# Decays between the tokens of a chunk from running sums in a hybrid encoder block

## Chip, cores and metric

The kernel runs on one core of a Trainium2 chip. The metric is the device time of one execution in microseconds; the median of three runs is given. TensorE (PE in the profile) multiplies matrices into PSUM, VectorE (DVE), ScalarE (ACT) and GpSimd (POOL) work elementwise, and the queue of SyncE (SP) issues nearly all DMAs.

## What is computed

The reference is an encoder block for 2048 tokens of 1024 channels with two branches: a gated delta rule in both directions, and a long convolution. The change is in the delta rule. Per head and direction, g is the running sum of the tokens' log decays within a chunk, and every pair of tokens i >= j of the chunk has the decay exp(g_i - g_j):

```python
g = jnp.cumsum(g..., axis=-1)
diff = g[..., :, None] - g[..., None, :]
decay = jnp.where(tril, jnp.exp(jnp.where(tril, diff, 0.0)), 0.0)
a = jnp.where(strict, jnp.einsum("nhcid,nhcjd->nhcij", k_beta, k) * decay, 0.0) + eye
sol = triangular_solve(a, [v * beta, k_beta * exp(g)])
attn = jnp.einsum("nhcid,nhcjd->nhcij", q, k) * decay
# then a scan over the chunks with the state S: v_new = u - w S, o = q S + attn v_new, S = S g_last + k^T v_new
```

## The kernel before

All large products are f32 split into two parts (h and l, `fp32r`), three products each. The program goes through the normalised input, the second branch's projections with its filter, the gates (`gates_in`), the projections of the delta rule (`delta_in`), the merge gates (`gate_out`), the recurrence over the chunks (`chain`) and the output projections.

Projections: `products` (L595) makes one block of 128 columns for 512 tokens with 24 products of 128x512. A head of `delta_in` has three blocks of four quarters, 288 products. After each product `tick` advances a generator, the filler, once per `gran` products (8 in `delta_in` up to its last blocks, 4 behind them), and `wait(n)` lets at least n products pass. From `gates_in` on, TensorE executes this hand-written order; the other engines' orders are a scheduler's.

The filler there is `delta_prep`. For each of 8 heads it runs `corr`, `invert32` and `invert`, up to three heads at a time in turn; a head starts when its projections are done and `corr` of the head before is through. `corr` takes four groups of four chunks of 128 tokens. Per group: products of keys with keys (`pka`) and queries with keys (`pkb`, L899); diagonal and step sizes on VectorE (L905 to L911); then for both directions the decay `e`, which is multiplied with beta on GpSimd (`co`, L923) and with `pka` on VectorE (L924), cut into blocks and stored, masked on GpSimd (L933), multiplied with `pkb` on VectorE (L935) and stored. `e` itself is made of two masked copies of the decays, `gmh` on GpSimd and `gml` on VectorE (L915), a pause of 12 products, two products with a triangle of ones (`pd`, L919) that add the decays from j to i, and an exponential on ScalarE (L921). `invert32` inverts 32x32 blocks on VectorE (L954, L956), one row after the other. `invert` puts them together to chunks with five groups of products per four chunks (L992 to L1021), whose results go through `ptw` (ScalarE), `G`, `T` (VectorE) and copies on either (`evac`).

When the filler is through or a block of `gate_out` ends behind it, `chain` becomes the filler, at the same kind of pace over the remaining blocks of `gate_out`.

Of the kernel before, what the change touches and what calls it, by code (L numbers as in the profile page):

```python
# [11 lines left out]
F32 = mybir.dt.float32  # L12
# [10 lines left out]
H = 8  # L23
# [3 lines left out]
# per direction: (source, target) blocks of 32 rows, and halves of 64  # L27
# [54 lines left out]
def _consts():  # L82
# [70 lines left out]
class Ring:  # L153
    """Tiles that are kept for the whole phase and used in turn."""
# [11 lines left out]
class K:  # L166
# [13 lines left out]
    def tick(self):  # L180
        """Called per matrix product; work of the filler goes between the products."""
# [42 lines left out]
    def sin(self, pool, y):  # L224
        """y -> y reduced to [-pi, pi], in place."""
# [121 lines left out]
    def filt_freq(self, pp, rk_dram, kf_dram):  # L347
        """Spectrum of the filter, real parts over imaginary parts, one slot after the other."""
# [29 lines left out]
    def conv_freq(self, pp, ru_dram, kf_dram, r2_dram):  # L378
        """Product of the spectra and the way back to rows, N channels at a time."""
# [6 lines left out]
        with tc.tile_pool(name="cf", bufs=1) as cp:  # L386
# [3 lines left out]
            def fetch(i):  # L390
# [14 lines left out]
                else:  # L405
                    # row 0 of the first slot holds two real values
# [127 lines left out]
    def start(self, sz_dram, consts):  # L534
        """The normalised input, each part of the tokens used as soon as it is there."""
# [30 lines left out]
    def z_out(self, pool, h, q, ps, sz_dram):  # L566
        """silu(z) * norm weight."""
# [16 lines left out]
    def proj(self, pp, w, q):  # L584
        """One block of 128 columns for 512 tokens: [columns, tokens] in PSUM."""
# [12 lines left out]
    def conv_in(self, pool, tag, prev, ps, q, cw, out):  # L598
        """Takes a quarter out of PSUM; returns its tile and finishes the quarter before it."""
# [18 lines left out]
    def quarters(self, wp, pp, pool, src, cw, tag, done, w=None):  # L618
        """Projection and short convolution of one block; done(q, tile) gets each quarter."""
# [831 lines left out]
```

## Time and profile before

| | before |
|---|---|
| time, median of 3 runs | 3622.15 us (3622.11 to 3626.81) |
| profiled execution, span | 3631.3 us |
| busy: TensorE, VectorE, ScalarE, GpSimd | 94%, 61%, 39%, 42% |
| TensorE's granted clock, mean | 0.973 of 2.4 GHz |

The profiled execution is one run of the program; its span runs from its first to its last instruction. A busy time is the time in which at least one instruction of the engine is running. TensorE's products overlap, so a product's recorded duration is longer than its distance to the next one. A wait is named by the instruction that waited and the one that released it.

### The profile page before, as it was taken

What the parts mean: (1) busy time and instruction counts of PE and PEld (TensorE: products, weight loads), DVE (VectorE), ACT (ScalarE), POOL (GpSimd) and SP (SyncE); (2) the same over time, 40 slices, a digit from 0 to 9 for tenths busy, and PEclk for the clock granted to TensorE, in tenths of its full rate; (3) what the DMA queues carried; (4) which work ended last, traced back from release to release, by engine and by line L of the source; (5) the groups of instructions that cost most, each with busy time, mean ns of one, the idle gap of its engine ahead of it and who ended that gap; (6) DMA issues with size and microseconds to landing.
All of it is one profiled execution on the core that took longest, in us unless ns stands there. A gap on an engine that the chain in (4) does not pass through costs nothing. (4 is left out here: it accounts for less than half of the span.)

```text
span 3631.3 us, 57914 instructions
## 1 busy us (share of the span) xinstructions
PE 3398.0 (94%) x18300; PEld 2870.9 (79%) x18300; DVE 2229.7 (61%) x4847; ACT 1415.6 (39%) x3425; POOL 1535.4 (42%) x1899
## 2 busy tenths in 40 slices
PE   7999999999999988889999989899998888998999
PEld 6768888888887767777777778788887766888998
DVE  7596566555325687798887652455555599535433
ACT  3344444443223434444443332344444577413221
POOL 3235666676432443433443222433334587324210
PEclk9999999999999999999999999999999999999999
DMA  3343333475211345555555654676677688886442
GB/s 125 131 100 99 111 120 97 133 237 173 86 55 60 105 109 137 134 131 128 139 130 150 152 135 112 192 210 209 200 215 213 203 276 260 282 303 189 148 140 94
DMA packets 721609, 565.03 MB, mean 156 GB/s; under 512 B 251302, under 2 KB 616954, under 8 KB 720280
## 3 DMA queue, kind: packets, MB, share of 16 engines
q1 hardware_dynamic: 721160, 561.21, 53.7%
q8 instruction: 146, 2.39, 0.3%
q14 instruction: 159, 1.30, 0.1%
q0 software_dynamic: 144, 0.13, 0.0%
HBM read 342.96 MB, written 218.17 MB: 155 GB/s over the span
## 5 line engine op out<-in xcount | busy, mean ns | idle before, releaser
L595 PE MATMUL pj<-hh,wh 128*128 128x512 f32 (+1 forms) x2592 | 1042.8, 403 | 22.7 <-DVE wh L204 11.2
L595 PE MATMUL pj<-hl,wh 128*128 128x512 f32 (+1 forms) x2592 | 1039.7, 402 | 3.5 <-POOL hl L205 2.9
L595 PE MATMUL pj<-hh,wl 128*128 128x512 f32 (+1 forms) x2592 | 1038.9, 402 | 1.3 <-POOL wl L205 1.2
L595 PEld LDWEIGHTS pj<-hh,wh 128*128 128x128 f32 x2592 | 498.6, 193 | 116.4 <-DVE wh L204 13.3
L595 PEld LDWEIGHTS pj<-hl,wh 128*128 128x128 f32 x2592 | 499.0, 193 | 91.9 <-POOL hl L205 3.6
L595 PEld LDWEIGHTS pj<-hh,wl 128*128 128x128 f32 x2592 | 498.5, 192 | 91.6 <-issue 4.4
L205 POOL TENSOR_TENSOR wl<-wraw,wh 128x512 fp32r<-128x512 f32 x160 | 221.3, 1383 | 395.9 <-DVE wh L204 261.0
L1084 POOL TENSOR_SCALAR kvq<-kvq,kn 128x128 f32<-128x128 f32 x256 | 153.9, 610 | 300.0 <-DMA kvq<-kvq 81.5
L204 DVE CAST wh<-wraw 128x512 fp32r<-128x512 f32 x160 | 89.4, 559 | 158.2 <-DMA wraw<-in_wb 106.8
L1304 POOL TENSOR_TENSOR gt<-gt,ex 128x256 f32<-128x256 f32 x64 | 48.0, 750 | 190.1 <-issue 98.8
L915 POOL TENSOR_TENSOR gmh<-masks,gh 128x512 fp32r<-128x512 f32 x64 | 75.0, 1172 | 124.6 <-PE pd L919 108.1
L209 PE MATMUL pj<-rh,hh 128*128 128x256 f32 x448 | 126.7, 284 | 1.0 <-DVE gt L1303 0.9
L210 PE MATMUL pj<-rl,hh 128*128 128x256 f32 x448 | 126.8, 283 | 0.6 <-POOL rl L205 0.6
L211 PE MATMUL pj<-rh,hl 128*128 128x256 f32 x448 | 126.7, 283 | 0.0
L616 DVE SCALAR_TENSOR_TENSOR o<-h_p,chy,o 128x512 f32<-128x512 f32 x96 | 83.1, 876 | 70.7 <-POOL h_p L608 69.5
L1164 DVE SCALAR_TENSOR_TENSOR S<-S,gt,ch 128x128 f32<-128x128 f32 x224 | 69.1, 344 | 93.4 <-PE ch L1161 93.2
L205 POOL TENSOR_TENSOR fl<-f,fh 128x256 fp32r<-128x256 f32 x128 | 99.5, 781 | 61.1 <-DVE fh L204 61.0
L205 POOL TENSOR_TENSOR l<-raw,h 128x256 fp32r<-128x256 f32 x128 | 99.9, 793 | 42.2 <-DVE h L204 41.9
L205 POOL TENSOR_TENSOR hl<-oraw,hh 128x512 fp32r<-128x512 f32 x48 | 62.5, 1304 | 130.5 <-ACT hh L202 116.5
L204 DVE CAST h<-raw 128x256 fp32r<-128x256 f32 x128 | 68.1, 547 | 75.0 <-PE pk L211 50.8
L927 ACT ACTIVATE od<-co 32x128 f32<-32x128 f32 x256 | 78.5, 307 | 88.1 <-DVE co L924 74.6
L923 POOL TENSOR_TENSOR co<-e,beta 128x512 f32<-128x512 f32 x64 | 79.5, 1242 | 73.4 <-ACT e L921 54.4
(328 smaller groups left out, 8145.7 us busy)
## 6 DMA issues: line engine op xcount, KB each, us to landing
kvq<-kvq SPq DMA_DIRECT2D x256, 192.0 KB
wraw<-in_wb SPq DMA_DIRECT2D x160, 256.0 KB
ep<-ep SPq DMA_DIRECT2D x256, 128.0 KB
ru<-ev SPq DMA_DIRECT2D x64, 256.0 KB
rk<-ev SPq DMA_DIRECT2D x128, 128.0 KB
raw<-rk SPq DMA_DIRECT2D x128, 128.0 KB
kf<-ev SPq DMA_DIRECT2D x128, 128.0 KB
kvq<-th SPq DMA_DIRECT2D x64, 256.0 KB
```

The costliest lines, as they stand in the source:

```text
L204: (eng_h or nc.vector).tensor_copy(h, src)
L205: (eng_l or nc.gpsimd).tensor_tensor(l, src, h.bitcast(F32), op=ALU.subtract)
L209: nc.tensor.matmul(ps, lhsT=ah, rhs=bh, start=first, stop=False)
L210: nc.tensor.matmul(ps, lhsT=ah, rhs=bl, start=False, stop=False)
L211: nc.tensor.matmul(ps, lhsT=al, rhs=bh, start=False, stop=last)
L595: self.nc.tensor.matmul(ps, lhsT=a[:, k], rhs=b[k][:, ts_], start=k == 0 and j == 0, stop=k == 7 and j == 2)
L616: nc.vector.scalar_tensor_tensor(out, p[:, 2:514], cw[:, 2:3], out, op0=ALU.mult, op1=ALU.add)
L915: e.tensor_tensor(t, self.mi[d].rearrange("p (a b) -> p a b", a=1).broadcast_to(S4), col(v.bitcast(F32), d), op=ALU.mult)
L923: nc.gpsimd.tensor_tensor(o, e, col(self.an, d), op=ALU.mult)
L927: nc.scalar.activation(od[blk(b)], o[blk(b), :, blk(b)], AF.Copy)
L1084: nc.gpsimd.tensor_scalar(a[:, 1], a[:, 1], self.kn[:, h, c:c + 1], None, op0=ALU.mult)
L1164: nc.vector.scalar_tensor_tensor(Sn, St[d], self.gt[:, c, ci], ps[:, 2], op0=ALU.mult, op1=ALU.add)
```

## The change

`gates_in` now makes the running sums of the decays of all heads, chunks and both directions with one product each against the constant `mid` (sums counted from the middle token of the chunk), keeps them with tokens on partitions (`cum`), turns them, and stores them in DRAM (`cr`), one row of 128 tokens per chunk. In `corr`, `decay(g, d)` loads four chunks' rows to all 128 partitions, clips -(row - cum) at zero on ScalarE, one chunk per instruction since `cum` differs by chunk, and takes exp(-x). The decays of the first group are asked for before the head's first products, those of group g + 1 right behind the last use of those of group g. `e` has three buffers instead of one; the PSUM buffer of `pd` becomes a second one for the inversions. The masked copies, the products `pd` and the pause ahead of them are gone; the pause between the directions is 12 products instead of 1. The masks and g stay in plain f32.

```diff
+    c["mid"] = np.stack([le - le[:, 63:64], le.T - le.T[:, 64:65]], 1)
...
+            mid = dp.tile([128, 2, 128], F32, name="mid", bufs=1)
+            self.load(mid, A["mid"])
+            ps = tp.tile([128, 2, H, NCH], F32, name="pcum", tag="pt")
+            for d in range(2):
+                nc.tensor.matmul(ps[:, d], lhsT=mid[:, d], rhs=self.g[:, :, 8 * d:8 * d + 8].rearrange("p c h -> p h c"), start=True, stop=True)
+            nc.scalar.activation(self.cum, ps, AF.Copy)
+            pt = tp.tile([128, 2, 128], F32, name="pcr", tag="pt")
+            for d in range(2):
+                nc.tensor.transpose(pt[:, d], self.cum[:, d].rearrange("p h c -> p (h c)"), self.ident)
+            cr = dp.tile([128, 2, 128], F32, name="cr", bufs=1)
+            nc.scalar.activation(cr, pt, AF.Copy)
+            self.store(cr_dram.rearrange("d r t -> r d t"), cr)
...
-        self.split(self.gh, self.gl, y, eng_l=V)
+        V.tensor_copy(self.g, y)
...
+        def decay(g, d):
+
+            e = P.tile(S4, F32, name="e", bufs=3)
+            rows = cr[d, NCH * h + 4 * g:NCH * h + 4 * g + 4].rearrange("(a c) t -> a (c t)", a=1)
+            self.load(e.rearrange("p c t -> p (c t)"), rows.broadcast_to([128, 512]))
+            for j in range(4):
+                nc.scalar.activation(e[:, j], e[:, j], AF.Relu, scale=-1.0, bias=self.cum[:, d, h, 4 * g + j:4 * g + j + 1])
+            nc.scalar.activation(e, e, AF.Exp, scale=-1.0)
+            return e
...
             if g == 0:
                 kq = fetch(0)
+                es = [decay(0, d) for d in range(2)]
                 yield from self.wait(36)
...
             for d in range(2):
-                gm = [P.tile(S4, F32R, name=n) for n in ("gmh", "gml")]
-                for t, v, e in zip(gm, (self.gh, self.gl), (nc.gpsimd, nc.vector)):
-                    e.tensor_tensor(t, self.mi[d].rearrange("p (a b) -> p a b", a=1).broadcast_to(S4), col(v.bitcast(F32), d), op=ALU.mult)
-                yield from self.wait(12)
-                pd = pp.tile(S4, F32, name="pd", tag="fc")
-                for i, t in enumerate(gm):
-                    nc.tensor.matmul(pd, lhsT=self.msr[:, d], rhs=t, start=i == 0, stop=i == 1)
-                e = P.tile(S4, F32, name="e")
-                nc.scalar.activation(e, pd, AF.Exp)
+                e = es[d]
...
-                yield from self.wait(28 if d else 1)
+                if g < 3:
+                    es[d] = decay(g + 1, d)
+                yield from self.wait(28 if d else 12)
...
-            ps = pp.tile([128, 4, 32], F32, name="l32", tag="lv")
+            ps = pp.tile([128, 4, 32], F32, name="l32", tag="lv", bufs=2)
```

In the order of the built programs, counted in projection products from the program's start, the heads' first key products stand here (the recurrence's first at 6916 in both, with as many blocks of `gate_out` left):

| head | 0 | 1 | 2 | 3 | 4 | 5 | 6 | 7 |
|---|---|---|---|---|---|---|---|---|
| before | 3960 | 4296 | 4632 | 4968 | 5304 | 5640 | 5952 | 6280 |
| after | 3960 | 4248 | 4536 | 4824 | 5112 | 5400 | 5688 | 6280 |
| after, inversion's first product | 4392 | 4680 | 4968 | 5256 | 5544 | 5832 | 6068 | 6632 |

A group of four chunks takes 72 products before and 48 after (with a `gran` of 8), 56 and 40 at a `gran` of 4. The sums' products in `gates_in` stand at 3718 and 3739.

TensorE, in head 1's key products, between the same projection products (`hh`, `hl`: the input's parts; `wh`, `wl`: a weight's). Before:

```order
L595 MATMUL pj<-hl_135,wh 128x512
L595 MATMUL pj<-hh_119,wl 128x512
L595 MATMUL pj<-hh_120,wh 128x512
L919 MATMUL pd<-gmh,msr 128x512
L919 MATMUL pd<-gml,msr 128x512
L595 MATMUL pj<-hl_136,wh 128x512
L595 MATMUL pj<-hh_120,wl 128x512
```

After:

```order
L597 MATMUL pj<-hl_135,wh 128x512
L597 MATMUL pj<-hh_119,wl 128x512
L597 MATMUL pj<-hh_120,wh 128x512
L597 MATMUL pj<-hl_136,wh 128x512
L597 MATMUL pj<-hh_120,wl 128x512
L597 MATMUL pj<-hh_121,wh 128x512
L1030 MATMUL l_14451<-masks,G 128x128 x4
```

The two products of the decay are gone, and the inversion of the head before has moved up to this place.

ScalarE, in the same part (`d_p`, `d_o`: a projection out of PSUM for the short convolution; `th`: its SiLU; `od`: diagonal blocks of `co`; `ptw`: the inversion's first product). Before:

```order
L927 ACTIVATE od<-co 32x128 x4
L602 ACTIVATE d_p<-pj 128x512
L603 ACTIVATE d_o<-pj,cdn 128x512
L767 ACTIVATE th<-d_o 128x512
L921 ACTIVATE e<-pd 128x512
```

After:

```order
L946 ACTIVATE od<-co 32x128 x4
L911 ACTIVATE e<-e,cum 128x128 x4
L604 ACTIVATE d_p<-pj 128x512
L605 ACTIVATE d_o<-pj,cdn 128x512
L912 ACTIVATE e<-e 128x512
L1015 ACTIVATE ptw<-l_15785 32x4x32 x4
```

Four clips per decay have come in, ahead of copies out of PSUM.

SP, in the same part (`c`: blocks of `co` for the inversion, `dg`: its diagonal blocks, `kvq`: keys, queries, values). Before:

```order
L177 DMA c_0_77<-co 32x4x32 x2
L177 DMA dg_72<-od 128x4x32
L177 DMA c_0_80<-co 64x4x64
L177 DMA ep_94<-e 128x4x128
L177 DMA kvq_88<-th 128x4x128
```

After:

```order
L179 DMA c_0_80<-co 64x4x64
L179 DMA dg_72<-od 128x4x32
L179 DMA ep_94<-e 128x4x128
L176 DMA Ca<-c_2_79 128x512
L176 DMA e<-cr 128x512
L179 DMA kvq_87<-th 128x4x128
```

The load of the next rows has come in behind the store of a decay and an inversion's load.

## Rows read from the trace of the kernel before

**Rows 1.** Page, busy us of each engine, share of the span, instructions
```profile
PE 3398.0 (94%) x18300; PEld 2870.9 (79%) x18300; DVE 2229.7 (61%) x4847; ACT 1415.6 (39%) x3425; POOL 1535.4 (42%) x1899
```

**Rows 2.** Stretches, us; busy PE, PEld, DVE, ACT, POOL (instructions), PEclk, DMA share, GB/s
```profile
1299.00:1942.00 643.00, 573.58 (x2906) 473.57 (x2905) 532.73 (x1187) 266.02 (x609) 252.67 (x324) 0.95 0.54 130
1942.00:2064.00 122.00, 110.83 (x581) 92.77 (x580) 94.44 (x249) 37.54 (x101) 34.57 (x33) 0.96 0.60 149
2064.00:2272.00 208.00, 197.02 (x1008) 165.87 (x1007) 84.98 (x231) 55.25 (x143) 58.03 (x41) 0.96 0.52 126
```

**Rows 3.** Waits of TensorE, 1299 to 2272 us: us in total, times, longest
```profile
PE l L1009 <- DVE T L1005: 27.5, 12, 4.7
PE l L1003 <- ACT ptw L994: 18.7, 10, 4.2
PE pka L899 <- DVE co L924: 10.5, 8, 2.6
```

**Rows 4.** Timeline of TensorE: start, us, instruction
```profile
1303.85 0.39 PE L595 MATMUL pj<-hl,wh 128*128 128x512 f32 x1
1304.07 0.39 PE L595 MATMUL pj<-hh,wl 128*128 128x512 f32 x1
1304.30 1.05 PE L899 MATMUL pka<-ka 128*128 128x128 f32 x8
1305.19 1.06 PE L899 MATMUL pkb<-qa,ka 128*128 128x128 f32 x8
```

**Rows 5.** Groups by line, 1299 to 2272 us: busy us, mean ns, idle before
```profile
L919 PE MATMUL pd<-gmh,msr 128*128 128x512 f32 x56 | 23.8, 425 | 3.3 <-POOL gmh L915 3.3
L919 PE MATMUL pd<-gml,msr 128*128 128x512 f32 x56 | 23.0, 411 | 1.1 <-DVE gml L915 1.1
L915 DVE TENSOR_TENSOR gml<-masks,gl 128x512 fp32r<-128x512 f32 x55 | 58.0, 1055 | 6.8 <-PE pd L919 6.4
L915 POOL TENSOR_TENSOR gmh<-masks,gh 128x512 fp32r<-128x512 f32 x55 | 64.8, 1179 | 111.5 <-PE pd L919 95.1 <-DMA ka<-kvq 11.5 <-DVE rk L908 4.9
L921 ACT ACTIVATE e<-pd 128x512 f32<-128x512 f32 x56 | 33.5, 598 | 125.5 <-PE pd L919 72.4 <-DMA ep<-e 46.3 <-PE l L1009 4.0
```

**Rows 6.** Groups by line, VectorE, 1299 to 1942 us
```profile
L615 DVE SCALAR_TENSOR_TENSOR d_o<-d_p,cdn,d_o 128x512 f32<-128x512 f32 x68 | 59.0, 867 | 0.9 <-ACT d_o L603 0.7
L616 DVE SCALAR_TENSOR_TENSOR d_o<-d_p,cdn,d_o 128x512 f32<-128x512 f32 x68 | 55.0, 818 | 2.7 <-POOL d_p L608 2.1
L768 DVE SCALAR_TENSOR_TENSOR th<-th,d_o 128x512 f32<-128x512 f32 x68 | 54.6, 808 | 3.5 <-ACT th L767 2.9
L204 DVE CAST wh<-wraw 128x512 fp32r<-128x512 f32 x36 | 21.1, 586 | 8.7 <-DMA wraw<-in_wb 6.1 <-PE pj L595 2.4
L205 DVE TENSOR_TENSOR sl<-th,sh 128x512 fp32r<-128x512 f32 x24 | 19.4, 808 | 0.1
L757 DVE COPY sq<-tv 128x512 f32<-128x512 f32 x23 | 15.7, 682 | 0.1
L204 DVE CAST sh<-th 128x512 fp32r<-128x512 f32 x24 | 14.2, 590 | 5.7 <-POOL th L774 5.6
```

**Rows 7.** Instructions of line 915, VectorE: ns min/median/max, first and last start
```profile
L915 DVE TENSOR_TENSOR gml<-masks,gl x64: 661/938/1760, 1146.7 to 2139.6; 128x512 fp32r<-128x512 f32 x64
```

**Rows 8.** Instructions of line 1108, ScalarE, columns as above
```profile
L1108 ACT ACTIVATE o<-o,sc x128: 384/390/421, 2337.0 to 2858.9; 128x128 f32<-128x128 f32 x128
```

**Rows 9.** Timeline, one load of 256 KB and the instruction that waits for it
```profile
1231.06 0.34 SPq L174 DMA_DIRECT2D wraw<-in_wb  x1
1235.01 0.43 DVE L204 CAST wh<-wraw 128x512 fp32r<-128x512 f32 x1 [1.70 <-DMA wraw<-in_wb]
```

**Rows 10.** Instructions of line 728, TensorE
```profile
L728 PE MATMUL pjb<-hl,wba x32: 389/392/479, 1085.1 to 1101.3; 128*64 128x512 f32 x32
```

**Rows 11.** Timeline of VectorE, the decays g are complete
```profile
1145.36 0.29 DVE L204 CAST gh<-sb 128x256 fp32r<-128x256 f32 x1
```

**Rows 12.** Instructions of line 572, VectorE
```profile
L572 DVE TENSOR_SCALAR th<-th,dnw x32: 471/486/2681, 52.6 to 2053.5; 128x512 f32<-128x512 f32 x32
```

More of the change, by code (lines that the diff above doesn't have):

```diff
@@ L712, in hyena_in, with gates_in @@
                 self.later.pop(0)()
-    def gates_in(self, pp, tp):
+    def gates_in(self, pp, tp, cr_dram):
         nc, tc, A = self.nc, self.tc, self.A
@@ L867, in delta_scalars @@
         self.beta = self.an = pool.tile(S, F32, name="beta")
-        self.gh, self.gl = [pool.tile(S, F32R, name=n) for n in ("gh", "gl")]
+        self.g = pool.tile(S, F32, name="g")
+        self.cum = pool.tile([128, 2, H, NCH], F32, name="cum")
         self.ss = pool.tile([128, H, NCH], F32, name="ss")
@@ L871, in delta_scalars, with corr @@
         self.nc.vector.tensor_copy(self.onesr, self.ones[:, 0:1])
-        self.msr = pool.tile([128, 2, 128], F32R, name="msr")
-        self.nc.gpsimd.dma_start(out=self.msr, in_=self.A["masks"][:, 0:2])
-    def corr(self, P, pp, h, kvq, dg, c32, c64, ep):
+        self.msr = pool.tile([128, 2, 128], F32, name="msr")
+        self.load(self.msr, self.A["masks"][:, 0:2])
+    def corr(self, P, pp, h, kvq, dg, c32, c64, ep, cr):
         nc = self.nc
@@ L1000, in invert @@
             yield from self.wait(6)
-            ps = pp.tile([128, 4, 32], F32, name="l32", tag="lv")
+            ps = pp.tile([128, 4, 32], F32, name="l32", tag="lv", bufs=2)
             for c in range(4):
@@ L1006, in invert @@
             yield from self.wait(6)
-            ps = pp.tile([128, 4, 128], F32, name="l64", tag="lv")
+            ps = pp.tile([128, 4, 128], F32, name="l64", tag="lv", bufs=2)
             for c in range(4):
@@ L1012, in invert @@
             yield from self.wait(6)
-            ps = pp.tile([128, 4, 128], F32, name="l64", tag="lv")
+            ps = pp.tile([128, 4, 128], F32, name="l64", tag="lv", bufs=2)
             for c in range(4):
@@ L1018, in invert @@
             yield from self.wait(6)
-            ps = pp.tile([128, 4, 64], F32, name="l64", tag="lv")
+            ps = pp.tile([128, 4, 64], F32, name="l64", tag="lv", bufs=2)
             for c in range(4):
@@ L1030, in invert, with delta_prep @@
             yield from self.wait(6)
-    def delta_prep(self, pp, kvq, dg, c32, c64, ep, nf, tf, ready):
+    def delta_prep(self, pp, kvq, dg, c32, c64, ep, nf, tf, cr, ready):
         nc = self.nc
@@ L1043, in head @@
                 a, b = h % 2, h % n
-                yield from self.corr(P, pp, h, kvq, dg[a], c32[b], c64[b], ep[h])
+                yield from self.corr(P, pp, h, kvq, dg[a], c32[b], c64[b], ep[h], cr)
                 free.append(h)
@@ L1065, in chain @@
         nc.gpsimd.tensor_tensor(self.kn, self.ss, self.kn, op=ALU.pow)
-        g = P.tile([128, NCH, 16], F32, name="g", tag="o", bufs=6)
-        nc.vector.tensor_tensor(g, self.gh.bitcast(F32), self.gl.bitcast(F32), op=ALU.add)
+        g = self.g
         for d in range(2):
             ds_ = slice(8 * d, 8 * d + 8)
-            for m, o in ((self.mi[d], self.eg), (self.msr.bitcast(F32)[:, d], self.es), (self.ones, self.gt)):
+            for m, o in ((self.mi[d], self.eg), (self.msr[:, d], self.es), (self.ones, self.gt)):
                 ps = pp.tile([128, NCH, 8], F32, name="cs", tag="tr")
@@ L1325, in run @@
             sqd = T("sqd", H, L)
+            cr = T("cr", 2, H * NCH, 128)
             zeros = [(t[:, 4 * g:4 * g + 4], slice(0, 128), 128) for t in c32 + c64 for g in range(4)]
@@ L1358, in run @@
                             self.delta_scalars(rpool(name="sc"))
-                            self.gates_in(pp, tp)
+                            self.gates_in(pp, tp, cr)
                             with tc.tile_pool(name="fp2", bufs=1, space=PSUM, **rt) as fp, tc.manual_schedule(engines=PE):
                                 ready = set()
-                                prep = self.delta_prep(fp, kvq, dg, c32, c64, ep, nf, tf, ready)
+                                prep = self.delta_prep(fp, kvq, dg, c32, c64, ep, nf, tf, cr, ready)
                                 self.filler = prep
```

## Prediction

> **What bounds the kernel now.** The page first: TensorE is busy for 94% of the span, VectorE for 61%, ScalarE for 39% [rows 1]. The change touches only what is done per head between the first product of the decays and the start of the recurrence, so I read that part next, in three stretches [rows 2]: heads 1 to 5 (1299 to 1942 us), head 6 (to 2064) and head 7 (to 2272, where the recurrence begins). In the first, TensorE is busy for 573.6 of 643 us while VectorE stands at 83%, ScalarE at 41%, GpSimd at 39%; the granted clock is 0.95, so about a tenth of the stretch runs at 1.2 GHz, the lower of the two levels, and the rest at 2.4. The three stretches hold 92 us in which TensorE is idle (973 - 881). The list of its waits says on whom: VectorE's copies of the inversions 27.5 us, ScalarE's 18.7, VectorE's products with the keys 10.5 [rows 3]. TensorE executes an order written by hand and comes to a row whose operand isn't out of the other engines' queues yet. So each microsecond of TensorE work taken out here shortens the span, and beside that there are up to 92 us of idle time, and the slow clock around it, that a lighter VectorE could give back.
>
> **The pace of a head.** By the order a head takes 336 projection products before and 288 after, in the dense part. A product takes 0.225 us at the full clock (three starts in 0.45 us), and the eight records of four f32 products 0.89, or 0.111 each [rows 4]. At that pace a head costs before: 336 x 0.225 = 75.6; 16 decay products x 0.225 = 3.6; 64 records of key products and 144 of the inversion x 0.111 = 23.1; column sums and turns of the projections some 4.2; together 106.5 us. The first stretch is 1680 products, five heads, in 643 us: 128.6 us each [rows 2]. The loss is 22.1 us a head, a factor of 1.21. VectorE is busy 106.5 us a head in it, just TensorE's own sum: neither has room, and that is why the loss is there.
>
> **What goes.** On TensorE the 128 products of line 919: 128 x 0.225 = 28.8 us. (Their recorded 0.41 to 0.43 us each overlap.) On VectorE 64 gml of 1.055 us, on GpSimd 64 gmh of 1.179, on ScalarE nothing: the exponential of 0.598 us stays and reads SBUF instead of PSUM [rows 5]. A head has eight of each (four groups, two directions), so VectorE gets back 8 x 1.055 = 8.4 us a head; at its best a gml takes 0.661 [rows 7], so 5.3 is the lower bound.
>
> **What the shorter pauses do.** A head's products after are 288 x 0.225 = 64.8, with 23.1 for keys and inversion and 3.6 for the rest: 91.5 us. VectorE's: 106.5 - 8.4 - the projections' own work of 48 products. That work is the seven groups of the projections, 239 us for 68 quarters of 24 products [rows 6], so two quarters are 7.0: 91.1 us. VectorE is as full beside TensorE as it was (91.1 to 91.5 against 106.5 to 106.5). The relief is eaten by the closer packing, so I keep the factor: 91.5 x 1.21 = 110.5 us a head. The dense part starts 48 products earlier (1299 - 10.8 = 1288) and holds six heads: 1288 + 663 = 1951. From there 964 products to the recurrence, which begins at the same product in both: 217 us, head 6's inversion 16, head 7's products 23, and the losses of the third stretch as they are (11 idle, 4% of 208 for the clock: 19): 275. Head 0 saves 16 products, 3.6. The recurrence starts at 1951 + 275 - 4 = 2222 in place of 2272: **50 us earlier**. Behind it the order is the same, with the same pauses, and I count nothing.
>
> **What is added.** ScalarE clips four pieces of 128x128 per decay, with a scalar per partition: the nearest row is line 1108, the same shape in place, 0.390 us [rows 8]. 64 x 4 x 0.39 = 100 us on ScalarE; its share in the dense part goes from 266/643 = 41% to (266/5 + 12.5)/110.5 = 59%. Of TensorE's waits 18.7 us are for ScalarE; growing with that share they become 27: **8 us back**. The bounds are 0 (all under projections, whose PSUM has three buffers; ScalarE is only given work, so no gain) and 100 (each clip in TensorE's way).
> The rows' loads: 64 of 256 KB on SP. A load of that size took 3.95 us from issue to the instruction that waited, and 0.34 to issue [rows 9]. Each is issued right behind the store of the decay of the group before, one group ahead of its use, so 48 products or 11 us cover it; its buffer is the third back, whose store has had a group's time too. Behind it on SP stand the next loads of weights and the inversions' stores, which lose 64 x 0.34 = 22 us of issue spread over 930. If a load is late, the first clip waits at the head of ScalarE's queue, and behind it stand the copies of the projections out of PSUM and ptw, for which TensorE waits. I take 0 (below 0 it can't be, nothing is taken off these queues); the upper bound is rival D's. DMA engines are at 0.54 to 0.60 [rows 2].
> At the gates: four small products, and the first needs the finished decays. The first product stands 166 projection products behind the last gate product at 1101.3 [rows 10], so not before 1101.3 + 37.4 + 3.6 for 32 small records = 1142; the decays are complete at 1145.4 [rows 11]. So TensorE waits 0 to 4 us; with 1 us for the products I take **1**. The second buffer for the inversions' PSUM counts 0: no wait in [rows 3] is for a buffer, all are for data. So does the rest: one masks load goes from GpSimd's queue to SP, two splits of g become one copy.
>
> **Sum.** -50 + 8 + 1 = -41 us. The profiled execution has 3631.3 us, 0.25% over the median; the difference is carried to the median: 3622 - 41 = **3581 us**.
>
> **A rule that speaks against the change.** The row: a VectorE instruction with one scalar per partition over 128x512 takes 0.486 us [rows 12], 31 us for 64, against 100 on ScalarE, but VectorE has no room. The Trainium skill, ScalarE: Activation LUTs, section Rules for kernel authors, says that relu, max and min belong on VectorE and not on ScalarE. By the rule 31 us would do in place of 100; by the rows they would lie on the engine that TensorE waits for most (27.5 against 18.7). I go by the rows; no run here shows the other placement.
>
> **The rivals.**
> *VectorE comes free (A).* The decay is ready before the keys' products, so GpSimd's and VectorE's chain no longer waits for products of TensorE and an exponential (gmh alone stood 95 us until the products had read the one before [rows 5]), and gml was stretched, 0.661 us at best and 0.938 in the median [rows 7]. If the loss factor falls to 1.10, six heads give 6 x 91.5 x 0.11 = 60 us more: 3521. Against it: VectorE's sum equals TensorE's. The Trainium skill, GPSIMD Engine Reference, section 1. Specifications, states that GpSimd shares its SBUF interfaces with VectorE; the stretched gml agrees, and by it gmh's end is worth up to its 1.179 us each to VectorE, 9 us a head, which would be this case.
> *Only the products (B).* The closer packing costs what VectorE's relief gives: 28.8 us and no more, 3593.
> *Nothing is left (C).* The products' waits for the inversions grow since one head's inversion now lies on the next one's small blocks, both on VectorE: a factor of 1.28 instead of 1.21 costs 6 x 91.5 x 0.07 = 38 us: about 3619.
> *ScalarE's queue (D), slower.* Clips wait in order for loaded rows, and behind them stand the copies out of PSUM that TensorE waits for; a load behind a blocked SP comes late. Of 64 decays each microsecond that reaches TensorE costs 64 us. From 0.125 us in my sum it decides at 0.125 + 41/64 = 0.77 us each; if the clips' whole 1.56 us reach it, 3581 - 8 + 100 = 3673. For it: ScalarE's wait is already second in the list. Against: 41% of it idle after, and the loads are a group ahead.
> That the change doesn't do what it says is out: the order shows the 128 products gone.
>
> **How the numbers follow.** Forecast 0.50 (its own range 3560 to 3600), A 0.15, B 0.15, C 0.08, D 0.12. Forecast, A and B are faster by over 0.2% (below 3615; 0.2% is about what a measurement here can tell): 0.80. C is within 0.2%: 0.08. D slower: 0.12. For eight in ten I leave out the far half of A and most of D: 3535 to 3625.
>
> **What would show it.** In the changed profile: no line 919; the recurrence's first product at about 2230 us; heads 1 to 6 at some 112 us each, VectorE still above 80% there. TensorE's waits for ScalarE up by no more than 10 us. Idle time of 40 us or less in the dense part speaks for A, waits of ScalarE for the loaded rows and of TensorE for ScalarE above 50 us for D. I am wrong if the end moves by much more or less than the recurrence's start does.

## The result

The changed kernel takes 3580.56 us (median of 4 runs, 3576.65 to 3590.7) beside 3623.46 us for the kernel before (4 runs on the same chip): a ratio of 0.9891, 95% interval 0.9872 to 0.9909, 42 us less at the medians. Forecast were 3581 us and "faster". Its profiled execution has a span of 3589.0 us, 42.3 less than before's 3631.3.

The page of the changed kernel, busy time of each engine; it answers to [rows 1]:

```profile
PE 3367.5 (94%) x18178; PEld 2848.8 (79%) x18178; DVE 2150.7 (60%) x4781; ACT 1491.0 (42%) x3683; POOL 1451.7 (40%) x1834
```

The same three stretches as in [rows 2], by this kernel's times (heads 1 to 5, head 6, head 7 up to the recurrence):

```profile
1297.00:1852.00 555.00, 493.68 (x2564) 406.63 (x2562) 457.09 (x1102) 299.39 (x746) 185.84 (x264) 0.96 0.66 163
1852.00:2054.00 202.00, 189.82 (x1009) 158.53 (x1009) 127.19 (x314) 76.67 (x199) 44.05 (x52) 0.98 0.59 146
2054.00:2228.00 174.00, 170.34 (x845) 143.61 (x845) 60.59 (x179) 47.09 (x122) 47.16 (x32) 0.99 0.52 142
```

Five heads take 555 us, 111.0 each, where they took 643 (128.6 in [rows 2]; 127.0 by the distance of their key products, which the table below uses; the fifth head of the kernel before has only 312 projection products ahead of the next one's keys, the other four 336). VectorE is still busy for 82% of that (457.09/555). The recurrence's first products (tile `cs`: instructions, ns min/median/max, first and last start):

```profile
L1092 PE MATMUL cs<-g,masks x8: 272/275/378, 2228.4 to 2232.9; 128*128 128x128 f32 x8
```

Before:

```profile
L1072 PE MATMUL cs<-g,masks x8: 272/275/377, 2274.5 to 2279.0; 128*128 128x128 f32 x8
```

The recurrence now begins 46 us earlier, and the end comes 42 earlier. So the gain lies ahead of the recurrence. The part behind it takes 1356.8 us before and 1360.6 after; over the traces of all versions with the same order there it is 1344 to 1368 us, so a difference of a few us at the end of single traces says nothing.

Waits of TensorE between 1297 and 2228 us (us in total, times, longest), beside [rows 3]:

```profile
PE pka L926 <- DVE co L943: 24.0, 9, 7.2
PE l L1024 <- ACT ptw L1015: 16.1, 13, 2.3
PE l L1036 <- ACT Gt L1221: 11.2, 5, 3.1
PE l L1030 <- DVE G L1026: 7.7, 11, 1.6
PE l L1042 <- ACT p2w L1221: 3.4, 4, 1.2
```

(`Gt` and `p2w` are later steps of the inversion than `ptw`.) The wait for VectorE's copies out of the inversion's second product, named by `T` in [rows 3] and by `G` here (L1005 and L1026 are the same line of the program, which writes both), has fallen from 27.5 to 7.7. That of the key products for `co` has grown (10.5 to 24.0), and those for ScalarE together are 30.7 (16.1 + 11.2 + 3.4) where 18.7 stood. Groups of instructions in the same stretch (busy us, mean ns, idle before and what ended it), beside [rows 5]:

```profile
L911 ACT ACTIVATE e<-e,cum 128x128 f32<-128x128 f32 x212 | 67.8, 390 | 79.8 <-DMA e<-cr 71.4 <-DMA c<-co 4.0 <-DMA Dm<-tf 4.0
L912 ACT ACTIVATE e<-e 128x512 f32<-128x512 f32 x53 | 33.2, 626 | 1.0
L942 POOL TENSOR_TENSOR co<-e,beta 128x512 f32<-128x512 f32 x56 | 66.7, 1191 | 114.1 <-DVE beta L938 68.5 <-DMA c<-co 23.5 <-issue 12.2
```

A clip takes 0.390 us, as the nearest row said [rows 8]. Two things are new: ScalarE stands 71.4 us at the head of its queue with a clip that waits for its loaded row, and GpSimd's `co` no longer waits for an exponential but for the step sizes of its own group.

### The profile page after: what moved, and what is told of

It reads as the page before. It is cut to its first block, busy times and chain, and to the rows that moved or that the text cites. A ratio compares the mean times of both kernels' runs of the same rounds, so it can differ in the third digit from the quotient of the medians.

```text
span 3589.0 us, 57740 instructions
## 1 busy us (share of the span) xinstructions
PE 3367.5 (94%) x18178; PEld 2848.8 (79%) x18178; DVE 2150.7 (60%) x4781; ACT 1491.0 (42%) x3683; POOL 1451.7 (40%) x1834
## 4 chain that ended last, share of the span: by engine, by line
PE 54%; DMA 14%; DVE 11%; issue 4%; ACT 4%; POOL 3%; SPq 2%; DVEq 0%; POOLq 0%; ACTq 0%
PE pj L597 28%; PE pf L211 2%; PE pf L213 2%; PE pf L212 2%; DMA wraw<-in_wb 2%; DVE xi L977 1%; DVE tm L975 1%; PE ch L1169 1%; PE po L1189 1%; PE pj L213 1%; PE pj L212 1%; PE pj L211 1%; DMA e<-cr 1%; DMA r<-r 1%; PE ch L1181 1%
## 5 line engine op out<-in xcount | busy, mean ns | idle before, releaser
L1184 DVE SCALAR_TENSOR_TENSOR S<-S,gt,ch 128x128 f32<-128x128 f32 x224 | 69.3, 344 | 97.9 <-PE ch L1181 97.4
L911 ACT ACTIVATE e<-e,cum 128x128 f32<-128x128 f32 x256 | 81.9, 390 | 105.7 <-DMA e<-cr 97.3
```

The source lines that it names most:

```text
L911: nc.scalar.activation(e[:, j], e[:, j], AF.Relu, scale=-1.0, bias=self.cum[:, d, h, 4 * g + j:4 * g + j + 1])
L1184: nc.vector.scalar_tensor_tensor(Sn, St[d], self.gt[:, c, ci], ps[:, 2], op0=ALU.mult, op1=ALU.add)
```

## The experiments

Ratios are to the kernel before, run on the same chip; 0.001 is 3.6 us. The first three columns of numbers are per head over heads 1 to 5 (from head 1's first key product to head 6's: 1656 projection products in before, e6 and e1, 1440 in the others), from one profiled execution each. Leaving a part out lets the scheduler order the other engines anew: of the variants with the changed kernel's order of TensorE only e8 and e9 keep its order of ScalarE nearly as it was, while in e3, e4, e5, e10, e11 and e13 some two thirds of ScalarE's instructions stand in the same sequence.

| kernel | us a head | VectorE busy, us | TensorE idle, us | ratio to before |
|---|---|---|---|---|
| before | 127.0 | 105.1 | 13.9 | 1 |
| e6, before without the 128 products | 121.7 | 99.6 | 13.0 | 0.9997 |
| e2, before at 48 products a group | 123.2 | 98.7 | 17.9 | 1.0175 |
| e1, changed at 72 products a group | 125.8 | 94.7 | 15.5 | 0.9989 |
| changed | 111.0 | 91.4 | 12.3 | 0.9891 |
| e13, small loads | 108.6 | 91.6 | 9.9 | 0.9806 |
| e3, clips on VectorE | 115.9 | 97.4 | 16.0 | 0.9958 |
| e12, changed at 40 products a group | 111.4 | 88.3 | 12.5 | 0.9936 |

### One part alone: the products, the pauses, the decays

**e6_before_no_pd**, the kernel before without the products of line 919:

```diff
-                pd = pp.tile(S4, F32, name="pd", tag="fc")
-                for i, t in enumerate(gm):
-                    nc.tensor.matmul(pd, lhsT=self.msr[:, d], rhs=t, start=i == 0, stop=i == 1)
...
-                nc.scalar.activation(e, pd, AF.Exp)
+                nc.scalar.activation(e, gm[1].bitcast(F32), AF.Exp)
```

> The kernel before without the 128 products of line 919: the exponential reads the masked copy gml in SBUF, so the sums of the decays are left out; copies and pauses stay. Theory: the products' own time lies on the path, 28.8 us: 3593 to 3597. Rival (VectorE sets the pace of the dense part and TensorE would only wait longer): 3612 to 3622. Rival (their end also takes the wait of the exponential for TensorE and of the copies for the products away): below 3580.

Measured: 3629.77 us, ratio 0.9997 (0.9986 to 1.0008). 28.8 us of TensorE's work taken away move the end by 1 us, give or take 4. On the prediction's scale that is 3621 us, in the range of the rival by which TensorE would only wait longer. Its profiled execution shows where some of it went: heads 1 to 5 are 26 us quicker (121.7 against 127.0 each), but head 0 takes 108 us instead of 96, with waits that are next to nothing before (3.2 us for `pss`, none for `pka`, 1100 to 1304 us), and the recurrence starts 11 us earlier (2263.8). Waits of TensorE, 1100 to 1324 us (`pss`: column sums of the projections):

```profile
PE pka L899 <- DVE co L921: 9.1, 2, 6.8
PE pss L746 <- DVE sh L204: 6.1, 1, 6.1
PE pss L747 <- DVE sl L205: 4.6, 3, 2.0
```

The experiment has a flaw of its own: `gml` now goes straight into the exponential, so VectorE's next `gml` waits for ScalarE. It shows that the products alone are not a gain in hand; it doesn't show that they were free in any surrounding.

**e2_before_48**, the kernel before with the pauses' sum of the changed one (48 products a group, the same order of heads). The old decay needs a pause of its own ahead of `pd`, so the 48 are spread otherwise: 16 ahead of either `pd` and 16 from the second one to the next group's keys, where the changed kernel has 16 between the directions and 32 to the next keys:

```diff
-                yield from self.wait(28 if d else 1)
+                if d:
+                    yield from self.wait(12)
```

> The kernel before with pauses that give it the order of the changed kernel: 48 products a group, 288 a head, the old decays kept. Theory: VectorE has 99.5 us a head against 95.1 of TensorE, so it is the bound and the packing brings nothing: about 120 us a head, 3622 to 3640 us. Rival (the packing itself shortens the span, since idle time of the light end is filled): 115 us a head, about 3609.

Measured: 3694.21 us, ratio 1.0175 (1.0162 to 1.0189), 63 us slower, more than either theory gave. Heads 1 to 5 are hardly quicker (123.2) although four of them hold 48 projection products less, and the fifth 24; these products must then be done later. TensorE waits in the place that shorter pauses would press on; its waits from 1310 to 1926 us:

```profile
PE pka L899 <- DVE co L924: 45.8, 11, 8.3
PE l L1016 <- DVE Gt L1204: 23.0, 5, 5.2
```

and a stretch's row of the same time, with the lowest granted clock of the table's kernels over these heads (0.92) and VectorE at 80%, less than before's 83%:

```profile
1310.00:1926.00 616.00, 526.33 (x2646) 436.21 (x2645) 493.65 (x1141) 253.70 (x586) 224.48 (x303) 0.92 0.55 130
```

The next group's keys wait for the PSUM buffer `pka`, which the second `co` of the group gives back. And `co` waits for the decay. GpSimd's group in the kernel before (1304 to 1939 us), in e2, and in the changed kernel (1297 to 1852 us), forty instructions each:

```profile
L923 POOL TENSOR_TENSOR co<-e,beta 128x512 f32<-128x512 f32 x40 | 51.1, 1277 | 33.4 <-ACT e L921 17.8 <-DVE tm L954 5.9 <-issue 3.5
```

```profile
L923 POOL TENSOR_TENSOR co<-e,beta 128x512 f32<-128x512 f32 x40 | 47.1, 1177 | 43.9 <-ACT e L921 39.9 <-issue 2.4 <-DMA ep<-T 1.0
```

```profile
L942 POOL TENSOR_TENSOR co<-e,beta 128x512 f32<-128x512 f32 x40 | 48.4, 1211 | 65.7 <-DVE beta L938 53.0 <-DMA c<-co 10.7 <-issue 1.9
```

17.8 us of waiting for the exponential with long pauses, 39.9 with short ones, none among the first three causes with decays that are made a group ahead. The old decay stands inside the group's chain from keys to `co`. In the first three groups of heads 1 to 5, the time from a group's first key product to the end of its second `co` on VectorE is 22.3 us in the median in before, 20.0 in e2 and 15.9 in the changed kernel, while 48 projection products are 10.8 us (48 x 0.225 [rows 4]). The next keys start within 0.5 us of that end in 6, 11 and 8 of these 15 groups. So at 48 products there is no time for the old decay, and the changed kernel's groups are paced in part by the chain that is left. How much of e2's 63 us is due to the way its 48 products are spread was not tried.

**e1_old_pauses**, the changed kernel with the pauses of before:

```diff
+                yield from self.wait(12)
...
-                yield from self.wait(28 if d else 12)
+                yield from self.wait(28 if d else 1)
```

> The changed kernel with the pauses of the kernel before (12, 1, 12, 28 products), so that a head again takes 336 projection products; only the way the decays are made differs from before. Theory (VectorE's fullness sets the loss): TensorE 102.9 us of products a head, VectorE 98.1, so the loss factor falls from 1.21 to about 1.13, some 116 us a head, and the recurrence starts near 2205 to 2215: 3560 to 3570 us. Rival (the shorter pauses bring most of the gain): about 3595 to 3605. Rival (the loss is the same 22 us a head whatever VectorE does): 125 us a head, about 3600.

Measured: 3623.71 us, ratio 0.9989 (0.9974 to 1.0003): with the long pauses the new decays bring nothing that shows at the end. Of the three ranges none held; the last rival's 125 us a head came, but not its time. VectorE is at 75% here (94.7 of 125.8 us a head), the products are gone, and yet a head takes only 1.2 us less than before. In its trace the recurrence starts 14 us earlier than before's (2260.7), and the part behind it takes 1368 us, the most of all traces with this order there. TensorE's waits, 1300 to 1950 us, the first two:

```profile
PE l L1025 <- ACT ptw L1016: 43.0, 14, 8.6
PE pss L761 <- DVE sh L206: 7.4, 4, 3.5
```

Here it waits for ScalarE's `ptw`, which stands in one queue with the clips; clips at its head wait 74.7 us for loaded rows in the same stretch. Whether the loads or the clips are why `ptw` is late in this kernel was not tried.

Together: the pauses alone, as e2 spreads them, cost 63 us, the decays alone gain 4 (-1 to 9), with the new loads and clips already paid, and both gain 39 by the ratio. The gain belongs to the pair, and the sum of the parts is far from it.

### The loaded rows

**e5_no_loads**, the changed kernel without the 64 loads; the clips read a resident tile:

```diff
-            rows = cr[d, NCH * h + 4 * g:NCH * h + 4 * g + 4].rearrange("(a c) t -> a (c t)", a=1)
-            self.load(e.rearrange("p c t -> p (c t)"), rows.broadcast_to([128, 512]))
...
-                nc.scalar.activation(e[:, j], e[:, j], AF.Relu, ...)
+                nc.scalar.activation(e[:, j], self.masks[:, j], AF.Relu, ...)
```

> The changed kernel without the 64 loads of rows: the clips read a tile of constants that lies in SBUF, so the decays are not those of the reference; clips, exponentials and order stay. In the changed kernel ScalarE waits 76 us for the rows in 44 waits. Sum of the prediction (loads are covered, cost 0): within 5 us of the changed kernel, 3576 to 3586. Rival D (late rows hold ScalarE's queue and TensorE behind it): 10 to 30 us faster, 3550 to 3570.

Measured: 3557.02 us, ratio 0.9802 (0.9789 to 0.9816), 0.0089 or 32 us below the changed kernel, give or take 8. So the loads, which the prediction counted at 0, bring a cost of that size with them. Three places could hold it: ScalarE's waits for rows, the issues on SP, the transfers. (The numbers that pass through the group differ too where the clips read constants, as in e5, e10 and e13, and so does the scheduler's order; neither was tried alone.)

**e9_loads_ahead**, each load asked for one direction earlier, clips where they were:

```diff
+                nx = rows(1, 0)
...
-                    es[d] = decay(g + 1, d)
+                    es[d] = decay(nx, g + 1, d)
+                    nx = rows(g + 1 + d, 1 - d) if g + d < 3 else None
```

> The changed kernel; each row load is asked for one direction earlier (its buffer, the third, is free by then), the clips and exponentials stay where they were in the program, TensorE's order is the same. Lateness theory: of the 105.7 us that ScalarE stood idle for the rows with a clip at the head of its queue, nearly all go, and with them most of the 24 us that the kernel without loads gained over the changed one (3557.0 against 3580.6): 3553 to 3568. Rival, traffic (the loads cost because they share the DMA engines and SP's queue with the weights): ScalarE's wait for rows falls just as far and the time stays at 3576 to 3586. A third outcome, that ScalarE's wait stays above 70 us, would say that the scheduler draws the clips forward with the loads, and tells nothing of the two.

Measured: 3590.55 us, ratio 0.9898 (0.9884 to 0.9911), the changed kernel's time, and ScalarE's wait for rows between 1200 and 2240 us is 89.0 us (92.2 in the changed kernel). It was the third outcome, and the starts in the two traces say why: loads and clips stand at the same places in both. In the changed kernel a load is issued 20.5 us ahead of GpSimd's use in the median (20.4 in e9; never less than 9.6 in either), its first clip starts 4.2 us behind the issue (4.1), where ScalarE mostly still waits for the landing, and the exponential ends 14.7 us ahead of the use (14.5; at least 3.0). Asking earlier moved nothing, since a load waits for its buffer (31 waits on SP for the store of a decay, 31.6 us in the changed kernel between 1200 and 2240 us). And the loads are covered: no `co` waits for its own rows. The clips are not late; they are early.

**e11_tied_clips**, clips held back, from the second group on, by a copy of their sums that VectorE can make only when the group before (or the group's step sizes) is through:

```diff
+                nc.vector.scalar_tensor_tensor(t, tie, 0.0, b, op0=ALU.mult, op1=ALU.add)
...
+            if g > 0:
+                decay(es[1], g, 1, rk)
...
+                if d == 1 and g < 3:
+                    decay(es[0], g + 1, 0, o[:, 0, 0:4])
```

> The changed kernel; loads as they were, but from the second group on the clips take their sums from a copy that VectorE makes only after the product of the group before (for the one direction) or after the step sizes of the group (for the other), so the scheduler can't put them right behind the load any more; first groups stay. 64 loads, 48 small copies of 128x4 more on VectorE (some 0.1 us each, an estimate, 5 us). Lateness theory: ScalarE's waits for rows, 92 us in the changed kernel between 1200 and 2240 us, fall below 40, and the time by most of the difference to the kernel without loads (0.9802 against 0.9891 of before, 32 us): ratio 0.980 to 0.985. Rival, traffic: the waits fall as far and the ratio stays at 0.987 to 0.991. A second rival: the clips now come so late that GpSimd's and VectorE's steps of the group wait for them: ratio above 0.992.

Measured: 3597.66 us, ratio 0.9915 (0.9897 to 0.9933), just above the traffic rival's range and far from the lateness theory's. ScalarE's waits, 1296 to 1858 us:

```profile
ACT od L959 <- DVE co L954: 67.3, 16, 8.0
ACT e L919 <- DVE cb L916: 18.8, 18, 2.3
ACT e L919 <- DMA e<-cr: 9.3, 6, 2.9
```

The wait for rows fell from 53.8 us in the changed kernel's stretch (1297 to 1852) to 9.3; half of it came back as waits for the copies (18.8), the engine waits longer for `co` (57.6 to 67.3), and a head takes 112.5 us instead of 111.0. Taking the waits away gained nothing, but since others took their place this run alone doesn't show that they were harmless; e13 bears on that.

**e10_dummy_loads**, no loads of rows, but 64 half loads into a tile that nothing reads:

```diff
+            dm = P.tile([128, 256], F32, name="dm")
+            self.load(dm, rows[:, 0:256].broadcast_to([128, 256]))
```

> The kernel without row loads (clips read a resident tile), with 64 loads of half the size, 128x256, into a tile that nothing reads: their issue on SP and half of their traffic come back, and no instruction waits for them. Lateness theory: as without loads, ratio 0.978 to 0.983. Traffic rival: half or more of the 32 us comes back, ratio 0.984 to 0.990.

Measured: 3617.9 us, ratio 0.9971 (0.9957 to 0.9984), outside both expectations, and inconclusive. Nothing but the one buffer holds these loads back, so all 64 were issued between 1158 and 1377 us, from the gates to head 1, each waiting on SP for the one before to land. SP's first wait between 1200 and 1470 us:

```profile
SPq L176 <- DMA dm<-cr: 93.6, 39, 4.5
```

Stretches of the same kernel, head 0, head 1 and the next four:

```profile
1223.00:1337.00 114.00, 81.81 (x378) 66.81 (x377) 67.69 (x146) 49.61 (x115) 36.60 (x54) 0.87 0.52 136
1337.00:1462.00 125.00, 97.09 (x488) 80.90 (x487) 94.97 (x232) 59.70 (x147) 41.04 (x55) 0.88 0.59 144
1462.00:1891.00 429.00, 393.61 (x2082) 325.85 (x2082) 359.04 (x874) 240.26 (x600) 149.98 (x209) 0.97 0.64 150
```

Its time tells of a blocked SP: head 0 starts 12 us later than in the changed kernel (1223.1 against 1211.3), heads 0 and 1 take 114 and 125 us (86.0 and 114.8 there), and then, without any such load, a head takes 107.

**e13_small_loads**, e5 with loads of 128x4 back, into the first columns of the tile that the clips then write: the same number of issues and of packets (731 thousand in the page of either kernel), 16.7 MB less to move. Of a decay's four clips only the one that writes these columns has to wait for the load; the scheduler put most of the others ahead of it:

```diff
+            rows = cr[d, NCH * h + 4 * g:NCH * h + 4 * g + 1, 0:4]
+            self.load(e[:, 0, 0:4], rows.broadcast_to([128, 4]))
```

> The kernel without row loads (clips read a resident tile), with 64 small loads, 128x4 in place of 128x512, into the tile that the clips then write: as many issues on SP, at the same places as in the changed kernel, and clips that wait for them; a hundredth of the traffic. Rows so far: taking ScalarE's waits for rows away left the time as it was, so the 24 to 33 us by which the kernel without loads is quicker are not these waits. If they are the traffic (packets that stand between those of weights and stores), the time is that without loads: ratio 0.977 to 0.983. If they are the issues on SP, 64 x 0.34 us, and what queues behind them: ratio 0.986 to 0.991, as the changed kernel. Between, both.

Measured: 3554.12 us, ratio 0.9806 (0.9782 to 0.983): the time without loads. Heads 1 to 5 and ScalarE's waits in them, 1290 to 1833 us:

```profile
1290.00:1833.00 543.00, 493.61 (x2566) 408.93 (x2565) 457.99 (x1103) 303.79 (x746) 188.72 (x263) 0.95 0.62 148
```

```profile
ACT e L912 <- DMA ep<-e: 39.0, 27, 4.1
ACT e L912 <- DMA e<-cr: 30.7, 25, 3.0
```

TensorE's waits for the inversion's copies, 1290 to 2205 us, and the recurrence's first products:

```profile
PE l L1037 <- ACT Gt L1222: 4.4, 6, 1.2
PE l L1031 <- DVE G L1027: 3.7, 7, 0.9
```

```profile
L1093 PE MATMUL cs<-g,masks x8: 272/276/377, 2204.6 to 2209.1; 128*128 128x128 f32 x8
```

TensorE's and VectorE's busy times are the changed kernel's (493.7 and 457.1); 12 us of idle time are gone (61.3 to 49.4). ScalarE waits even longer ahead of its clips, 69.7 us against 53.8 (39.0 of them for the store that frees the buffer), and the time is still that of e5: such waits at the head of its queue do no harm that shows (between 1200 and 2240 us they are 114.2 us in e13 and 54.4, for the store alone, in e5). The issues on SP are back and cost nothing that can be told from noise (some 10 us here). What is left is the transfers, 64 of 256 KB: about 31 us by the ratios (0.9891 - 0.9806), give or take 11; in the traces the recurrence starts 24 us earlier than in the changed kernel (2204.6). In the stretch the DMA share is 0.62 against 0.66. The granted clock isn't it (0.95 against 0.96). Which other transfer they hold up isn't shown: no wait for one grows by more than some 9 us between 1200 and 2240 us (ScalarE's for the stores of `G` 26.5 to 35.2, GpSimd's for those of `co` 16.6 to 24.0). Of TensorE's waits the inversion's shrink most, `Gt` from 11.2 to 4.4 us and `G` from 7.7 to 3.7 (1290 to 2205 us). So the transfers are found by elimination, and two rivals stay that were not tried by themselves: the scheduler's other order of ScalarE in e5 and e13, and the other numbers there. Against the first speaks that e11's order differs from the changed kernel's as much, with the loads in place, and is no quicker.

### The clips

**e4_no_clip**, the changed kernel without them:

```diff
-            for j in range(4):
-                nc.scalar.activation(e[:, j], e[:, j], AF.Relu, ...)
-            nc.scalar.activation(e, e, AF.Exp, scale=-1.0)
+            nc.scalar.activation(e, e, AF.Exp, scale=0.0)
```

> The changed kernel with the clips left out: the exponential reads the loaded rows with scale 0, loads stay. The prediction counted 8 us for the clips (bounds 0 and 100): 3573 by its own term, 3565 to 3581 as theory. Rival: the clips hold ScalarE's queue in TensorE's way for much of their 100 us: below 3555. Second rival: their time lies under other work and only the wait for rows counts, which the exponential now takes over: 3578 to 3585.

Measured: 3571.78 us, ratio 0.985 (0.9827 to 0.9872): 15 us below the changed kernel, give or take 11. 100 us of ScalarE's work cost 8 by the prediction, which the interval holds.

**e3_clip_vector**, the clips on VectorE:

```diff
-                nc.scalar.activation(e[:, j], e[:, j], AF.Relu, scale=-1.0, bias=...)
-            nc.scalar.activation(e, e, AF.Exp, scale=-1.0)
+                nc.vector.tensor_scalar(e[:, j], e[:, j], self.cum[...], 0.0, op0=ALU.subtract, op1=ALU.min)
+            nc.scalar.activation(e, e, AF.Exp)
```

> The changed kernel with the 256 clips on VectorE (subtract and min with a scalar per partition) in place of ScalarE; loads and exponentials as they were. By the rule weighed in the prediction (relu belongs on VectorE): ScalarE loses 100 us of work and the waits at the head of its queue, VectorE gains 256 pieces at 0.17 to 0.29 us (row of 128x128 with PSUM: 0.287), 44 to 74 us: 3560 to 3575. By the prediction's rows (VectorE is the engine that TensorE waits for, and its queue would now wait for the loaded rows): 5 to 9 us more a head on VectorE and the 76 us wait for rows moved onto its queue: 3600 to 3640.

Measured: 3614.19 us, ratio 0.9958 (0.9944 to 0.9972), 24 us slower than with the clips on ScalarE. Groups, 1297 to 2240 us:

```profile
L911 DVE TENSOR_SCALAR e<-e,cum 128x128 f32<-128x128 f32 x212 | 48.5, 288 | 51.4 <-DMA e<-cr 37.6 <-DMA Sm<-nf 7.6 <-DMA ep<-G 3.6
L912 ACT ACTIVATE e<-e 128x512 f32<-128x512 f32 x53 | 33.4, 631 | 93.3 <-DVE e L911 89.9 <-DMA qa<-kvq 2.8
```

TensorE's waits, 1290 to 2240 us:

```profile
PE pka L926 <- DVE co L943: 41.1, 14, 10.6
PE l L1030 <- DVE G L1026: 26.9, 13, 4.9
```

A clip is quicker on VectorE (0.288 us against 0.390), but it takes 48.5 us of work and 37.6 us of waiting for rows to the engine that releases TensorE's key products and inversions: the two waits are 41.1 and 26.9 us where 24.0 and 7.7 stood. The run doesn't part the work from the waiting.

### The second PSUM buffer, and shorter groups still

**e8_one_buffer**, `bufs=1` for the inversions' PSUM as before (the same edit in all five places):

```diff
-            ps = pp.tile([128, 4, 32], F32, name="l32", tag="lv", bufs=2)
+            ps = pp.tile([128, 4, 32], F32, name="l32", tag="lv", bufs=1)
```

> The changed kernel with one PSUM buffer for the inversions, as before. The prediction counted the second buffer at 0, since no wait of TensorE there was for a buffer: 3576 to 3586. Rival: with the inversions lying closer to the next head's small products the second buffer is part of the gain: 3590 or more.

Measured: 3588.48 us, ratio 0.9894 (0.9879 to 0.9908), as the changed kernel (0.9891); the kernel before took 3626 us on this chip.

**e12_40**, `wait(20 if d else 12)`, 40 products a group:

```diff
-                yield from self.wait(28 if d else 12)
+                yield from self.wait(20 if d else 12)
```

> The changed kernel with 16 and 24 products between the directions and groups, 40 per group and 256 a head in place of 48 and 288. If the pace of a head follows from its products with the loss factor of the prediction (1.21): 8 us a head less for six heads, 3580 - 52 = 3528 to 3550 or, with a growing factor, no worse than 3575. Theory from the kernel of before at 48 products (64 us slower): a group has a chain through GpSimd, VectorE and ScalarE of fixed length, and where the next group's keys come sooner than it ends, TensorE waits at the key products and falls to the slow clock: 3600 or more, with the wait of the key products for VectorE's co above 60 us (24 to 30 now).

Measured: 3604.84 us, ratio 0.9936 (0.9915 to 0.9957), 16 us slower than at 48. The time is in the second theory's range, but its sign is not there (the key products wait for `co` 40.2 us between 1200 and 2240, not above 60), and the first theory couldn't have held: a head's projections are 288 products, the next head starts with them, so a head can't hold fewer. It takes 111.4 us, as at 48; the small products only stand closer together within it. The recurrence starts 96 projection products earlier in this order (21.6 us at 0.225), but only 4 us earlier in time (2224.5), so the end isn't a pure comparison of the dense part.

None of these versions beats the changed kernel with the work complete.

## Why the prediction was right, and where only its sum was

**What bounds the kernel** held: the gain is TensorE's, made ahead of the recurrence. From product 3960 to the recurrence, 1064.0 us became 1015.4. TensorE's busy time fell by 38.0 (970.2 to 932.2), its idle time by 10.6 (93.8 to 83.2). Stretches at 1.2 GHz shrank from 92.2 to 64.9 us, half of which difference, 13.7 us, can be part of the 38; the other 24 are near the 28.8 of the 128 products that went (4903 records became 4775). But "each microsecond of TensorE work taken out here shortens the span" was too much: e6 took 28.8 out, and the end stayed.

**The pace of a head** was right in size and not in cause. Predicted 110.5 us, measured 111.0; "some 112" and "VectorE above 80%" (82%) too. But the reason given, that neither VectorE nor TensorE has room, doesn't hold. e1 takes VectorE from 83% to 75% and a head takes 125.8 us; e2 has VectorE at 80% and is the slowest of all; e13 has it at 84% and is the quickest. What the traces point to is a chain through queues in order, keys, step sizes, decay, `co`, next keys (22.3 us before, 15.9 after), whose length against the products laid over it decides whether TensorE waits. How much of the loss it makes isn't shown: in e1 no key product waits for `co`, and TensorE waits for `ptw` instead.

**"The relief is eaten by the closer packing, so I keep the factor"** is the step that failed. Without the loads' transfers (e13) the six heads of 288 products, 1290.5 to 1938.7 us, take 108.0 us each with their clips, where 110.5 and 8 us for all clips were counted, and the recurrence starts at 2204.6 us, where the sum gives 2231 (2222 + 9): the relief was larger than the kept factor of 1.21 allows. With the transfers back the six heads take 111.0 us each. A smaller slip lies behind them: from product 4248 six heads of 288 end at 5976, so 940 products are left to the recurrence and not 964, 5 us less.

**The loads at 0** is the term that was wrong by most, about 31 us (24 in the traces). The prediction asked whether a load is covered and whether its wait blocks a queue; the starts in the traces show that it is covered, and e13 that the wait is harmless. It didn't ask what 16 MB more do to DMA engines that stood at 0.54. These two errors, 26 and 24 us in the traces and of opposite sign, are why 3581 came out so close: the number is luck in part, and better than the argument.

**The products' 28.8 us** were counted on the path. In the changed kernel's own account TensorE's work is down by 24 us; taken alone they moved the end by 1 (e6). A term of a sum isn't what its part brings alone.

**ScalarE's clips at 8** (e4: 15, give or take 11), **the second buffer at 0** (e8) and **nothing behind the recurrence** (1356.8 us before, 1360.6 after, a difference within the traces' scatter) held. TensorE's waits for ScalarE grew by 12 us, where "no more than 10" stood. The 1 us at the gates is below what these profiles resolve: product 3960 starts at 1210.5 before and between 1209 and 1225 in the others.

**The rule against the change.** The Trainium skill, ScalarE: Activation LUTs, section Rules for kernel authors, puts relu, max and min on VectorE. e3 is the other placement: the instruction is quicker there, as the rule has it, and the kernel 24 us slower. The measurement decides for ScalarE in this kernel, by the rows the prediction went by.

**The rivals.** A (VectorE comes free): its sign, 40 us of idle time or less in the dense part, isn't there (61.3 in 555 us). Its time of 3521 lies below even the kernel without the transfers. What A drew from the end of `gmh`, up to 9 us a head for VectorE, isn't seen: VectorE is busy for 91.4 us a head, where 91.1 were counted without it. B would end at 28.8 us of gain, and e6 shows that these products alone are no gain in hand. C needs a loss factor of 1.28, and the changed kernel has 1.21 (111.0/91.5). D (ScalarE's queue): half of its sign is there, 71.4 us of ScalarE's waits for rows, and the other half isn't (TensorE waits for ScalarE 30.7 us, not above 50). e13 shows why: those waits didn't pass on. D's place for the cost was wrong; that the loads cost something was right.

## What to carry to other kernels

A step that stands in the chain between two uses of one buffer limits how close these uses can be placed; take it out of the chain first, then shorten the distance, and measure both together, since here the one alone gained 4 us (-1 to 9) and the other lost 63. A wait at the head of an in-order queue is to be priced by who waits for what stands behind it: 70 us of it were harmless on ScalarE, while the clips on VectorE, work and waits together, cost 24. A covered load need not be free: count its bytes against what the DMA engines already carry.

## What was not expected of the hardware

- 64 loads of 256 KB, whose rows were through clip and exponential at least 3.0 us ahead of their use (14.7 in the median), went with about 31 us of 3580, at a DMA share of 0.66 instead of 0.62; 64 loads of 2 KB, as many issues and packets, cost nothing that can be told from noise (0.9806 against 0.9802). The scheduler's order differs too, and which other transfer is held up isn't shown.
- A clip of 128x128 with a scalar per partition takes 0.390 us on ScalarE and 0.288 on VectorE.
- Loads that write one buffer in turn, with no reader, held SP's queue for 93.6 us in 39 waits, beside heads of 114 and 125 us (e10).
